# A hybrid decoder layer on one core: one tile of the input projection ahead of the first norm's spread

## The chip, the cores and the metric

The kernel runs on one core of one Trainium2 chip, as one program. The metric is the device time of one execution in microseconds (us). TensorE is called PE, VectorE DVE, ScalarE ACT, GpSimd POOL and SyncE SP.

## The reference, cut to what matters

One layer on 256 tokens of width 1024, in float32: a mixer whose three head groups read columns of one combined projection, then cross-attention to 256 memory tokens, then a gated feed-forward of width 2752 with a short convolution, and a last norm. The change touches the head and the tail of it:

```
def rmsnorm(x, g):
    xf = x.astype(jnp.float32)
    xf = xf * lax.rsqrt(jnp.mean(xf * xf, axis=-1, keepdims=True) + EPS)
    return xf.astype(x.dtype) * g
...
    proj = h @ w_in            # h = rmsnorm(x, norm_mix_g)
    (c_b, c_c, c_h, m_q, m_k, m_v, g_q, g_k, g_v, g_o, g_lr) = jnp.split(proj, points, axis=-1)
...
    return rmsnorm(x, final_norm_g)
```

## The kernel before, in words

Activations stand with features on the 128 partitions and the 256 tokens along the row. Each fp32 product is made from three: weights and activations are split into a high part (a cast to fp32r) and a low part (what is left), and PE adds high by high, high by low and low by high. ACT makes a weight's high part and DVE its low part (`emit_split`, lines 167 and 173; 162 and 163 where a piece is split in two halves).

All weights come as one stream of pieces in the order of `_stream_order`, loaded by `emit_load` on SP's queue into RAW = 6 raw buffers and split into PARTS = 4 pairs of buffers. The first eight pieces ("first", k) hold rows k of six column tiles of the input projection; PE works on all six at once, in the six PSUM tiles `first0` to `first5` (`fps`, line 295), while x arrives piece by piece. Pieces below HALVED = 3 are loaded, split and multiplied in two halves of 384 columns. The next pieces are single column tiles: ("in", MK+2P), here called in 1536 by its column, ("in", MQ+2P), in 1024, and then four "gla" pieces.

The norm's factor is not put into the operands; since it is one number per token, it is put into the results. It comes from a second load of x, token by token (`xtok`, 1 MB, line 237): ACT squares and sums it (line 345), `root_of` makes the root (lines 329, 330) and writes it on a diagonal (DVE, line 333), and `spread` (line 336) turns the diagonal with a matmul by ones into a row that every partition has, in the PSUM tile x_r, from which DVE copies it into `keep` (line 340). Only then can `scaled` (line 362) take a projection tile out of PSUM: `mk(0)` from first2, `mq(0)` from first3 and so on.

PSUM has eight banks here, in two tags, "ps" and "sd", of four each; `ps` (line 96) takes them by turns, and a new tile of a tag whose four banks are taken stands in the one that is released first. The warm-up tile, first0 to first5 and x_r take turns 1 to 8: warm, first1, first3 and first5 are "sd", first0, first2, first4 and x_r "ps". Then come in 1536 ("sd") and in 1024 ("ps").

A scheduler sets each engine's order from the program order and the dependencies, except where an instruction is pinned (`keep_in_program_order`, `manual_schedule`). Each engine and each DMA queue works in its order.

At the end, for each of two token tiles t, the last norm's factor r is put into the output row: DVE takes columns 512 to 1023 from PSUM (line 941), ACT columns 0 to 511 (line 944), each in two instructions of 256 columns, and SP and ACT each issue one store of 512 columns (line 946).

Of the kernel before, what the change touches and what calls it, by code (L numbers as in the profile page):

```python
# [14 lines left out]
AF = mybir.ActivationFunctionType  # L15
ALU = mybir.AluOpType
# [4 lines left out]
T = 256  # L21
D = 1024
KT = D // P
# [33 lines left out]

X_WITH = {1: (1, 2), 2: (2, 3), 3: (3, 4), 4: (4, 6), 6: (6, 8)}

HALVED = 3  # L60


def _stream_order():
# [14 lines left out]
def _width(key):  # L78
    return {"first": 768, "gla": 544}.get(key[0], 1024)
# [3 lines left out]
def trunk(ctx: ExitStack, tc: tile.TileContext, xT, x_rows, w_stream, params, gate, final, out):  # L83
    nc = tc.nc
    pe, act, dve, pool, sp = nc.tensor, nc.scalar, nc.vector, nc.gpsimd, nc.sync
# [10 lines left out]
    def ps(name):  # L96
        banks["turn"] += 1
        return pp.tile([P, 512], F32, tag=banks["tags"][banks["turn"] % len(banks["tags"])], name=name)

    def t1(name):  # L100
        return t1p.tile([P, T], F32, tag="t1", name=name)
# [18 lines left out]
    def emit_load():  # L120
        i = state["load"]
        state["load"] += 1
        key = order[i]
        t = rp.tile([P, SLOT], F32, tag="raw", name="w_" + "_".join(map(str, key)))
        if i == 0:

            act.dma_start(t[:, :384], w_stream[i, :, :384])
            load_x(0, 1)
            sp.dma_start(t[:, 384:768], w_stream[i, :, 384:768])
        else:  # L130
            if key[0] == "first" and key[1] in X_WITH:
                load_x(*X_WITH[key[1]])
            n = _width(key)
            step = n // 2 if i < HALVED else n
            for c in range(0, n, step):
                sp.dma_start(t[:, c:c + step], w_stream[i, :, c:c + step])
        raw[key] = t

    def emit_split(pin=False):
        i = state["split"]  # L140
        state["split"] += 1
        key = order[i]
        if key[0] == "mem":
            return
        n = _width(key)
        t = raw[key]
        if key in SPARE:
            tag = SPARE[key]
            if key[-1] == 0:
                spare[tag] = cp.tile([P, 4 * SLOT + 32], F32R, tag=tag, name="spare_" + tag)  # L150
            view = lambda c: spare[tag][:, ASIDE + c * SLOT:ASIDE + (c + 1) * SLOT]
            hi, lo = view(2 * key[-1]), view(2 * key[-1] + 1)
        elif key[0] == "dtail":
            hi = cp.tile([P, n], F32R, name="h_dtail")
            lo = lo_dtail
        else:
            at0 = 0 if key[0] in MOVING else ASIDE
            hi, lo = (hp.tile([P, SLOT + 32], F32R, tag=tag, name=tag[0] + "_" + "_".join(map(str, key)))[:, at0:at0 + n]
                      for tag in ("high", "low"))
        if i < HALVED:  # L160
            for c in (0, 384):
                act.copy(hi[:, c:c + 384], t[:, c:c + 384])  # L162
                dve.tensor_sub(lo[:, c:c + 384], t[:, c:c + 384], hi[:, c:c + 384])
            parts[key] = (hi, lo)
            return
        else:
            c = act.copy(hi, t[:, :n])  # L167
            if pin:
                tc.keep_in_program_order(c)
        if key[0] == "dtail":  # L170
            c = dve.tensor_sub(lo[:TAIL], t[:TAIL, :n], hi[:TAIL])
        else:
            c = dve.tensor_sub(lo, t[:, :n], hi)  # L173
        if pin:
            tc.keep_in_program_order(c)
        parts[key] = (hi, lo)

    def piece(*key):

        i = place[key]  # L180
        while state["load"] < min(len(order), i + RAW):
            emit_load()
        while state["split"] < min(len(order), i + 1 + AHEAD, state["until"]):
            emit_split()
        return raw[key] if key[0] == "mem" else parts[key]
# [31 lines left out]
    def feature_tile(dst, w, src, late=(), at=None, call=None):  # L217
        wb = blocks(w, P)
        ks = [k for k in range(KT) if k not in late]
        term = lambda k: ([a[:, k, :] for a in wb], [a[:, k, :] for a in src])  # L220
        todo = [(k, a, b) for g in (ks, late) for a, b in ((0, 0), (0, 1), (1, 0)) for k in g]
        for n, (k, a, b) in enumerate(todo):
            if n == at:
                call()
            s, m = term(k)
            pe.matmul(dst, s[a], m[b], start=(n == 0), stop=(n == len(todo) - 1))  # L226

    xt = cp.tile([P, PADDED + KT * T], F32, tag="res", bufs=2, name="x")
    x = xt[:, PADDED:].rearrange("p (k n) -> p k n", k=KT)
    emit_load()  # L230
    act.preload_act_table_set("natural_log_exp_and_others")
    for _ in range(KT - 1):
        emit_load()

    xtt = cp.tile([P, 4 * D], F32, tag="big", name="xtok")
# [9 lines left out]
    ones = cp.tile([P, P], F32, name="ones")  # L245
# [51 lines left out]
    with tc.manual_schedule(engines={mybir.EngineType.DVE}):  # L297
        for k in range(KT):
            state["until"] = place[("first", k)] + 1
            gained(xg, k, x[:, k, :], xt[:, k:k + 1], dve)  # L300
            w = piece("first", k)
            for some in ((range(3), range(3, 6)) if k < HALVED else (range(6),)):
                for a, b in ((0, 0), (0, 1), (1, 0)):
                    for i in some:
                        pe.matmul(fps[i][:, :T], w[a][:, i * P:(i + 1) * P], xg[b][:, k, :],  # L305
                                  start=(k == 0 and (a, b) == (0, 0)), stop=(k == KT - 1 and a == 1))
    state["until"] = place[("up", 0, 0)]

    def rstd_of(acc, name, features=True, tokens=False):


        m = ps(name + "_ms")
        got = []
        if features:
            pe.matmul(m[:, :T], ones, acc, start=True, stop=True)
            got.append((t1(name + "_r"), m[:, :T]))
        if tokens or not features:
            for j in range(2):
                pe.matmul(m[:, T + j:T + j + 1], acc[:, j * P:(j + 1) * P], ones[:, 0:1], start=True, stop=True)
            got.append((smp.tile([P, 2], F32, tag=name + "_rt", bufs=1, name=name + "_rt"), m[:, T:T + 2]))  # L320
        for r, q in got:
            act.activation(r, q, AF.Ln, bias=eps, scale=1.0)
            act.activation(r, r, AF.Exp, scale=-0.5)
        return [r for r, _ in got] if len(got) > 1 else got[0][0]

    def root_of(sums, name):

        rt = smp.tile([P, 2], F32, tag=name + "_rt", bufs=1, name=name + "_rt")
        act.activation(rt, sums, AF.Ln, bias=eps, scale=1.0 / D)
        act.activation(rt, rt, AF.Exp, scale=-0.5)  # L330
        diags = t1(name + "_diag")
        for j in range(2):
            dve.tensor_scalar(diags[:, j * P:(j + 1) * P], ident, rt[:, j:j + 1], float(D), op0=ALU.mult, op1=ALU.mult)
        return rt, diags

    def spread(r, diags, name):

        m = ps(name + "_r")
        pe.matmul(m[:, :T], ones, diags, start=True, stop=True)
        dve.tensor_copy(r, m[:, :T])  # L340

    xsum = small("x_sums")
# [3 lines left out]
    rt, diags = root_of(xsum, "x")  # L346
    keep = cp.tile([P, 2, T], F32, name="keep")
    rr, r = keep[:, 0, :], keep[:, 1, :]
    spread(r, diags, "x")


    for j in range(2):
# [15 lines left out]
    def dense(*key):  # L368
        q = ps("_".join(map(str, key)))
        feature_tile(q[:, :T], piece(*key), xg)  # L370
        return q[:, :T]
# [47 lines left out]
    def both(f, h):  # L419
        f(h)  # L420
        f(h + 1)

    both(bias_of, 0)
    q2 = dense("in", MK + 2 * P)
    gq, gk = t1("gq"), t1("gk")
    for i in range(2):
        scaled(mk(i), fps[2 + 2 * i][:, :T])
# [28 lines left out]
    for i in range(4):  # L456
        w = blocks(piece("gla", i), 272)
        for j in range(2):
            for a, b in ((0, 0), (1, 0), (0, 1)):
                for k in range(2):  # L460
                    pe.matmul(gps[j][:, :272], xg[a][:, 2 * i + k, j * P:(j + 1) * P], w[b][:, k, :],  # L461
                              start=(i == 0 and k == 0 and (a, b) == (0, 0)), stop=(i == 3 and k == 1 and b == 1))
# [135 lines left out]
    for n in (1, 2, 3):  # L598
        for c in range(2):
            ch = slice(64 * c, 64 * c + 64)  # L600
            pe.matmul(gos[c][:, 64 * n:64 * n + 64], st[ch, n, :], qd[ch, 64 * n:64 * n + 64],
                      start=False, stop=(n == 3), tile_position=(64 * c, 0))
# [157 lines left out]
    wps, acc = {}, {}  # L760
# [35 lines left out]
    gfin = cp.tile([P, D], F32, name="gfin")  # L796
# [58 lines left out]
    for j in range(NPAIR + 1):  # L855
        tail = j == NPAIR
        src = []
        for t in range(1 if tail else 2):
# [6 lines left out]
            elif t == 1:  # L865
# [3 lines left out]
                for k in range(KT):  # L869
                    for tt in range(2):  # L870
                        wb = blocks(piece("up", 0, tt), P)
                        for a, b in ((0, 0), (0, 1), (1, 0)):
                            pe.matmul(src[tt], wb[a][:, k, :], xg2[b][:, k, :], start=(k + a + b + tt == 0),
                                      stop=(k == KT - 1 and a == 1 and tt == 1))
# [4 lines left out]
                _, diags2 = root_of(tot2, "x2")  # L879
# [21 lines left out]
    fin = fint[:, :2 * D].rearrange("p (t n) -> p t n", t=2)  # L901
    half = fint[:, 2 * D:].rearrange("p (t n) -> p t n", t=2)
# [30 lines left out]
    for n, k, t in second:  # L933
        down(t, n, k)
        if k == NPAIR - 1:
            squares(t, 1)
            r = rs[:, t:t + 1]
            act.activation(r, sums[:, 2 * t + 1:2 * t + 2], AF.Ln, bias=bias[:, t:t + 1], scale=1.0 / D)
            act.activation(r, r, AF.Exp, scale=-0.5)
            for c in (512, 768):  # L940
                dve.scalar_tensor_tensor(fin[:, t, c:c + 256], acc[t, 1][:, c - 512:c - 256], r, gfin[:, c:c + 256],
                                         op0=ALU.mult, op1=ALU.mult)
            for c in (0, 256):
                act.activation(fin[:, t, c:c + 256], half[:, t, c:c + 256], AF.Copy, scale=r)
            for c, e in ((512, sp), (0, act)):
                e.dma_start(out[t * P:(t + 1) * P, c:c + 512], fin[:, t, c:c + 512])

# [99 lines left out]
```

## Time and profile before

| what | value |
|---|---|
| median of 3 runs | 330.21 us (330.07 to 331.2) |
| the profiled execution's own time | 330.21 us |
| its span, first to last instruction | 328.5 us |
| busy PE / DVE / ACT | 98% / 78% / 65% of the span |

The span is what the trace shows; the time has some 1.7 us around it. A row of the timeline gives the start, the time from there to the end of the last of its instructions, the engine and line, the operation, the tile written and the tiles read, and in brackets how long the engine sat idle before it and what ended that. A matmul's end is modelled, so PE's starts are what is read from it.

### The profile page before, as it was taken

The numbers are of one execution on the slowest core, as the hardware profiler recorded it, in microseconds if no ns is written. First come the engines' busy times: TensorE is split into PE (matmuls) and PEld (weight loads), VectorE is DVE, ScalarE is ACT, GpSimd is POOL, SyncE is SP. The second block draws the span as 40 slices with busy tenths as digits, with TensorE's granted clock in tenths as the row PEclk, the third lists the DMA queues.
The fourth block names the chain that finished last, engine by engine and source line by source line (L and its number), as shares of the span: only waits on it lengthen the run. The fifth ranks groups of instructions, "written<-read, shape, count | busy, mean of one in ns | idle before, by whom it ended". The sixth has DMA issues, their size and how long they took to land.

```text
span 328.5 us, 6408 instructions
## 1 busy us (share of the span) xinstructions
PE 320.3 (98%) x2462; PEld 296.2 (90%) x2462; DVE 257.2 (78%) x499; ACT 212.0 (65%) x393; POOL 2.7 (1%) x16
## 2 busy tenths in 40 slices
PE   8999999999999999999999999999999999999993
PEld 5999879898999998899999999999999988888882
DVE  7869879797998858588999999898989974444411
ACT  4675999566666756587886677666677653363323
POOL 3000000000000000000000000000000000000000
PEclk9999999999999999999999999999999999999999
DMA  7979953743378644207076866556558756552003
GB/s 218 401 302 323 325 188 89 247 177 131 130 234 274 198 130 129 66 0 257 0 224 229 272 228 203 194 192 195 193 192 246 210 182 200 192 191 66 0 0 128
DMA packets 18465, 60.38 MB, mean 184 GB/s; under 512 B 2034, under 2 KB 3459, under 8 KB 18435
## 3 DMA queue, kind: packets, MB, share of 16 engines
q1 hardware_dynamic: 18002, 59.26, 54.1%
q10 hardware_dynamic: 432, 0.72, 0.6%
q8 instruction: 19, 0.31, 0.4%
q14 instruction: 12, 0.09, 0.1%
HBM read 58.93 MB, written 1.05 MB: 183 GB/s over the span
## 4 chain that ended last, share of the span: by engine, by line
PE 85%; ACT 6%; DMA 4%; DVE 2%; issue 1%; SPq 0%; DVEq 0%; ACTq 0%
PE up L226 30%; PE dn L911 18%; PE in L226 10%; PE out L215 7%; PE v L477 3%; DMA xtok<-in_x_rows_dram 3%; PE gv L461 2%; PE xv L737 2%; PE wo L779 2%; PE xq L226 2%; PE xk L226 2%; ACT h_up L167 2%; DMA w_first<-in_w_stream_dram 1%; ACT hn L201 1%; PE et L404 1%; ACT x_sq L771 1%
## 5 line engine op out<-in xcount | busy, mean ns | idle before, releaser
L226 PE MATMUL up<-hn,h_up 128*128 128x256 f32 x576 | 71.2, 276 | 0.0
L226 PEld LDWEIGHTS up<-hn,h_up 128*128 128x128 f32 x576 | 68.0, 188 | 0.0
L167 ACT CAST h_up<-w_up 128x1024 fp32r<-128x1024 f32 x40 | 41.8, 1049 | 18.8 <-PE up L226 18.7
L911 PE MATMUL dn<-h_down,hid 128*128 128x512 f32 x168 | 52.8, 392 | 0.0
L173 DVE TENSOR_TENSOR l_up<-w_up,h_up 128x1024 fp32r<-128x1024 f32 x40 | 48.6, 1220 | 4.5 <-ACT h_up L167 3.6
L173 DVE TENSOR_TENSOR l_down<-w_down,h_down 128x1024 fp32r<-128x1024 f32 x21 | 25.7, 1225 | 25.2 <-ACT h_down L167 24.8
L167 ACT CAST h_down<-w_down 128x1024 fp32r<-128x1024 f32 x21 | 22.0, 1048 | 28.1 <-PE dn L911 25.2
L226 PE MATMUL up<-hn,l_up 128*128 128x256 f32 x288 | 38.6, 276 | 0.3 <-DVE l_up L173 0.3
L911 PEld LDWEIGHTS dn<-h_down,hid 128*128 128x128 f32 x168 | 31.6, 188 | 7.1
L226 PEld LDWEIGHTS up<-hn,l_up 128*128 128x128 f32 x288 | 35.4, 188 | 0.5 <-DVE l_up L173 0.5
L810 DVE SCALAR_TENSOR_TENSOR u<-up,par,u 128x255 f32<-128x255 f32 (+1 forms) x74 | 34.5, 476 | 0.5
L911 PE MATMUL dn<-l_down,hid 128*128 128x512 f32 x84 | 32.9, 392 | 0.0
L226 PE MATMUL in<-xg,h_in 128*128 128x256 f32 x192 | 25.0, 283 | 0.0
L226 PEld LDWEIGHTS in<-xg,h_in 128*128 128x128 f32 x192 | 23.0, 188 | 0.7 <-issue 0.5
L808 ACT ACTIVATE u<-up,par 128x256 f32<-128x256 f32 x37 | 20.5, 555 | 0.0
L911 PEld LDWEIGHTS dn<-l_down,hid 128*128 128x128 f32 x84 | 15.8, 188 | 3.5
L215 PE MATMUL out<-y,h_out 128*128 128x256 f32 x128 | 16.0, 277 | 0.0
L173 DVE TENSOR_TENSOR l_in<-w_in,h_in 128x1024 fp32r<-128x1024 f32 x12 | 14.6, 1220 | 1.7 <-ACT h_in L167 1.7
L215 PEld LDWEIGHTS out<-y,h_out 128*128 128x128 f32 x128 | 15.3, 188 | 0.0
L167 ACT CAST h_in<-w_in 128x1024 fp32r<-128x1024 f32 x12 | 12.4, 1044 | 3.9 <-issue 2.7
L305 PE MATMUL first<-xg,h_first 128*128 128x256 f32 x96 | 13.1, 280 | 0.8 <-ACT h_first L162 0.7
L305 PEld LDWEIGHTS first<-xg,h_first 128*128 128x128 f32 x96 | 11.8, 188 | 1.6 <-ACT h_first L162 1.3
(269 smaller groups left out, 543.6 us busy)
## 6 DMA issues: line engine op xcount, KB each, us to landing
w_up<-in_w_stream_dram SPq DMA_DIRECT2D x42, 512.0 KB, 3.4
w_down<-in_w_stream_dram SPq DMA_DIRECT2D x21, 512.0 KB, 3.3
w_in<-in_w_stream_dram SPq DMA_DIRECT2D x12, 512.0 KB, 4.7
w_out<-in_w_stream_dram SPq DMA_DIRECT2D x8, 512.0 KB, 3.4
w_mv<-in_w_stream_dram SPq DMA_DIRECT2D x4, 512.0 KB, 5.3
w_first<-in_w_stream_dram SPq DMA_DIRECT2D x5, 384.0 KB, 6.3
w_gla<-in_w_stream_dram SPq DMA_DIRECT2D x4, 272.0 KB, 6.7
xtok<-in_x_rows_dram SPq DMA_DIRECT2D x1, 1024.0 KB, 9.4
```

The lines of the kernel that those rows point to most:

```text
L167: c = act.copy(hi, t[:, :n])
L173: c = dve.tensor_sub(lo, t[:, :n], hi)
L215: pe.matmul(dst, s, m, start=(n == 0), stop=(n == len(todo) - 1))
L226: pe.matmul(dst, s[a], m[b], start=(n == 0), stop=(n == len(todo) - 1))
L305: pe.matmul(fps[i][:, :T], w[a][:, i * P:(i + 1) * P], xg[b][:, k, :], start=(k == 0 and (a, b) == (0, 0)), stop=(k == KT - 1 and a == 1))
L461: pe.matmul(gps[j][:, :272], xg[a][:, 2 * i + k, j * P:(j + 1) * P], w[b][:, k, :], start=(i == 0 and k == 0 and (a, b) == (0, 0)), stop=( ...
L477: pe.matmul(vps[j], xg[a][:, 2 * i + k, j * P:(j + 1) * P], w[b][:, k, :], start=(i == 0 and k == 0 and (a, b) == (0, 0)), stop=(i == 3 an ...
L737: pe.matmul(vps[j][:, :T], mg[a][:, 4 * i + k, j * P:(j + 1) * P], w[b][:, k, :], start=(i == 0 and k == 0 and (a, b) == (0, 0)), stop=(i ...
L779: pe.matmul(wps[o][:, :T], wb[a][:, 2 * (o % 4) + k, :], xo[b][:, k, :], start=(k == 0 and a + b == 0), stop=(k == 1 and a == 1))
L808: act.activation(v, src, AF.Identity, bias=fb(t), scale=fw(t, 2))
L810: dve.scalar_tensor_tensor(v[:, s:], src[:, :T - s], fw(t, 2 - s), v[:, s:], op0=ALU.mult, op1=ALU.add)
L911: pe.matmul(q, hid[i](k)[:, cols], w[j], start=False, stop=(k == NPAIR - 1 and i == 1), skip_group_check=True)
```

## The change

Four edits. The tile in 1536 is multiplied ahead of `spread`, whose matmul is now pinned to its place in the program; its weights are loaded ahead of `xtok` (nine loads are issued first, not eight) and split, pinned, ahead of the squares; HALVED is 4, so the fourth "first" piece is loaded, split and multiplied in halves; and the last results are written in one instruction of 512 columns on each engine.

```
-HALVED = 3
+HALVED = 4
...
-    for _ in range(KT - 1):
+    for _ in range(KT):
         emit_load()
...
     state["until"] = place[("up", 0, 0)]
+    emit_split(True)
...
-        pe.matmul(m[:, :T], ones, diags, start=True, stop=True)
+        tc.keep_in_program_order(pe.matmul(m[:, :T], ones, diags, start=True, stop=True))
...
-    spread(r, diags, "x")
...
     both(bias_of, 0)
     q2 = dense("in", MK + 2 * P)
+    spread(r, diags, "x")
...
-            for c in (512, 768):
-                dve.scalar_tensor_tensor(fin[:, t, c:c + 256], acc[t, 1][:, c - 512:c - 256], r, gfin[:, c:c + 256],
-                                         op0=ALU.mult, op1=ALU.mult)
-            for c in (0, 256):
-                act.activation(fin[:, t, c:c + 256], half[:, t, c:c + 256], AF.Copy, scale=r)
+            dve.scalar_tensor_tensor(fin[:, t, 512:], acc[t, 1], r, gfin[:, 512:], op0=ALU.mult, op1=ALU.mult)
+            act.activation(fin[:, t, :512], half[:, t, :], AF.Copy, scale=r)
```

On PE, from the last product of the first six tiles to the first scores, before (a name's number is its buffer; the tile behind the brackets' word is not told, only the engine whose semaphore is waited for):

```order
L305 MATMUL first5_165<-xg_159,l_first_7_355 128x256
L339 MATMUL x_r_387<-x_diag_383,ones_109 128x256 [waits DVE_49]
L226 MATMUL in_1536_398<-xg_159,h_in_1536_401 128x256 [waits Activation_49]
L226 MATMUL in_1536_398<-xg_159,h_in_1536_401 128x256 x15
L226 MATMUL in_1536_398<-xg_159,l_in_1536_402 128x256 [waits DVE_49]
L226 MATMUL in_1536_398<-xg_159,l_in_1536_402 128x256 x7
L226 MATMUL in_1024_447<-xg_159,h_in_1024_405 128x256 [waits DVE_49,Activation_49]
```

and now:

```order
L305 MATMUL first5_168<-xg_162,l_first_7_358 128x256
L226 MATMUL in_1536_402<-xg_162,h_in_1536_380 128x256 [waits Activation_49]
L226 MATMUL in_1536_402<-xg_162,h_in_1536_380 128x256 x15
L226 MATMUL in_1536_402<-xg_162,l_in_1536_381 128x256 [waits DVE_49]
L226 MATMUL in_1536_402<-xg_162,l_in_1536_381 128x256 x7
L340 MATMUL x_r_437<-x_diag_390,ones_112 128x256 [waits DVE_49,PE_49]
L226 MATMUL in_1024_450<-xg_162,h_in_1024_405 128x256 [waits DVE_49,Activation_49]
```

x_r's matmul has gone behind the 24 products of in 1536; in 1024 still waits for DVE, but its tile now has another predecessor in its bank. By the turns, in 1536 is now the fourth "ps" tile and x_r stands in the warm-up's "sd" bank, so in 1024 must take a "ps" bank from first0, first2, first4 or in 1536.

On DVE, from the last low part of the first pieces to the first scaled tiles, before:

```order
L173 TENSOR_TENSOR l_first_7_355<-w_first_7_101,h_first_7_354 128x768
L333 TENSOR_SCALAR x_diag_383<-ident_127,x_rt_380 128x128 x2
L173 TENSOR_TENSOR l_in_1536_402<-w_in_1536_248,h_in_1536_401 128x1024
L340 COPY keep_386<-x_r_387 128x256
L173 TENSOR_TENSOR l_in_1024_406<-w_in_1024_274,h_in_1024_405 128x1024
L173 TENSOR_TENSOR l_gla_0_410<-w_gla_0_300,h_gla_0_409 128x544
L364 TENSOR_TENSOR mix_392<-first2_162,keep_386 128x256
```

and now:

```order
L173 TENSOR_TENSOR l_first_7_358<-w_first_7_102,h_first_7_357 128x768
L173 TENSOR_TENSOR l_in_1536_381<-w_in_1536_104,h_in_1536_380 128x1024
L334 TENSOR_SCALAR x_diag_390<-ident_130,x_rt_387 128x128 x2
L173 TENSOR_TENSOR l_in_1024_406<-w_in_1024_277,h_in_1024_405 128x1024
L173 TENSOR_TENSOR l_gla_0_410<-w_gla_0_303,h_gla_0_409 128x544
L341 COPY keep_393<-x_r_437 128x256
L173 TENSOR_TENSOR l_gla_1_454<-w_gla_1_329,h_gla_1_453 128x544
L364 TENSOR_TENSOR mix_396<-first2_165,keep_393 128x256
```

The copy of x_r now stands behind the low parts of in 1024 and of the first gla piece, and the first scaled tile behind that of the second gla piece too.

On SP's queue, around the second load of x, before:

```order
L136 DMA w_first_7_101<-in_w_stream_dram 128x768
L237 DMA xtok_103<-in_x_rows_dram 128x2x1024
L239 DMA par_105<-in_params_dram 128x224
L241 DMA wg_107<-in_gate_dram 17x128
L136 DMA w_in_1536_248<-in_w_stream_dram 128x1024
```

and now:

```order
L136 DMA w_first_7_102<-in_w_stream_dram 128x768
L136 DMA w_in_1536_104<-in_w_stream_dram 128x1024
L237 DMA xtok_106<-in_x_rows_dram 128x2x1024
L239 DMA par_108<-in_params_dram 128x224
L241 DMA wg_110<-in_gate_dram 17x128
```

The 512 KB of in 1536 have gone ahead of xtok, the parameters and the gate's weights.

## Rows read from the trace of the kernel before

**Rows 1.** Page, part 1: busy time, share of the span, instructions.
```profile
PE 320.3 (98%) x2462; PEld 296.2 (90%) x2462; DVE 257.2 (78%) x499; ACT 212.0 (65%) x393; POOL 2.7 (1%) x16
```

**Rows 2.** PE's waits over the whole span: total us, times, longest.
```profile
PE warm L290 <- PEq L1035: 0.9, 1, 0.9
PE first L305 <- ACT h_first L162: 0.7, 1, 0.7
PE x_r L339 <- DVE x_diag L333: 0.4, 2, 0.2
PE up L226 <- DVE l_up L173: 0.3, 1, 0.3
```

**Rows 3.** Timeline of PE from 20.9 us.
```profile
21.11 0.84 PE L305 MATMUL first<-xg,l_first 128*128 128x256 f32 x6
22.15 0.70 PE L339 MATMUL x_r<-x_diag,ones 128*128 128x256 f32 x2 [0.19 <-DVE x_diag L333]
22.56 2.17 PE L226 MATMUL in<-xg,h_in 128*128 128x256 f32 x16
...
25.51 1.99 PE L226 MATMUL in<-xg,h_in 128*128 128x256 f32 x16
...
28.34 0.50 PE L385 MATMUL s<-mix 64*128 64x128 f32 x4
```

**Rows 4.** Timeline of ACT: x's second load has landed.
```profile
18.82 1.06 ACT L345 ACTIVATE xtok<-xtok 128x1024 f32<-128x1024 f32 x1 [2.21 <-DMA xtok<-in_x_rows_dram]
...
21.48 1.98 ACT L167 CAST h_in<-w_in 128x1024 fp32r<-128x1024 f32 x2
```

**Rows 5.** Timeline of DVE from 22.5 us.
```profile
22.54 1.22 DVE L173 TENSOR_TENSOR l_in<-w_in,h_in 128x1024 fp32r<-128x1024 f32 x1 [0.45 <-ACT h_in L167]
23.68 0.42 DVE L340 COPY keep<-x_r 128x256 f32<-128x256 f32 x1
24.02 1.22 DVE L173 TENSOR_TENSOR l_in<-w_in,h_in 128x1024 fp32r<-128x1024 f32 x1
25.15 0.72 DVE L173 TENSOR_TENSOR l_gla<-w_gla,h_gla 128x544 fp32r<-128x544 f32 x1
25.79 0.42 DVE L364 TENSOR_TENSOR mix<-first,keep 128x256 f32<-128x256 f32 x1
26.12 0.41 DVE L366 SCALAR_TENSOR_TENSOR mix<-first,keep 128x256 f32<-128x256 f32 x1
```

**Rows 6.** Stretches: length, PE, PEld, DVE, ACT, POOL busy; PEclk, DMA share, GB/s.
```profile
4.00:8.80 4.80, 4.08 (x34) 3.95 (x34) 4.51 (x12) 2.89 (x6) 0.00 (x0) 1.00 0.97 294
...
14.00:18.80 4.80, 4.80 (x45) 4.80 (x44) 4.70 (x10) 1.71 (x3) 0.00 (x0) 1.00 1.04 416
```

**Rows 7.** Timeline of ACT and of PE around the fourth piece.
```profile
10.58 0.83 ACT L167 CAST h_first<-w_first 128x768 fp32r<-128x768 f32 x1 [1.64 <-DMA w_first<-in_w_stream_dram]
...
10.89 0.50 PE L305 MATMUL first<-xg,l_first 128*128 128x256 f32 x3
11.47 1.65 PE L305 MATMUL first<-xg,h_first 128*128 128x256 f32 x12
```

**Rows 8.** The tail's timeline, and three groups of instructions (busy us, mean ns).
```profile
324.04 0.91 ACT L944 ACTIVATE fin<-fin,x_r 128x256 f32<-128x256 f32 x2
324.04 0.88 DVE L941 SCALAR_TENSOR_TENSOR fin<-dn,x_r,gfin 128x256 f32<-128x256 f32 x2 [3.25 <-ACT x_r L939]
...
L932 DVE TENSOR_TENSOR fin<-dn,gfin 128x512 f32<-128x512 f32 x2 | 1.4, 681 | 0.0
L503 ACT ACTIVATE mix<-v,x_rt 128x512 f32<-128x512 f32 x2 | 1.2, 669 | 0.0
L465 ACT ACTIVATE gv<-gv,x_rt 128x256 f32<-128x256 f32 x2 | 0.9, 461 | 0.0
```

**Rows 9.** Timeline of PE, the warm-up.
```profile
0.85 3.22 PE L290 MATMUL warm<-const-bfloat16-1.0 128*128 128x512 bf16 x8 [0.85 <-PEq L1035]
```

## The prediction

> **What bounds the kernel now.** I read the share of busy time first: PE is busy for 98% of the span, DVE for 78%, ACT for 65% [rows 1]. Then PE's own waits [rows 2]: apart from the start there are two, 0.4 us for the norm's diagonal (two records, 0.2 the longest) and 0.3 us once for a low part. So PE bounds nearly everything, a microsecond that PE loses near the head has nothing behind it that would give it back, and the change can win at most the small gap in front of x_r and something in the tail. That gap is read from starts [rows 3]: the last six products of the first tiles start at 21.11, and at 24 products in 2.83 us (25.51 to 28.34), 0.118 each, PE could go on at 21.82; x_r starts at 22.15. The gap is 0.33 us. What x_r waits for begins with xtok: ACT's squares start when it lands, at 18.82 [rows 4].
>
> A change of 0.5%, 1.65 us, is about what a measurement of this kernel can tell from none.
>
> **The fourth piece by halves.** PE runs out of the third piece's products at 10.89 + 3 × 0.118 = 11.24 and starts the fourth at 11.47, when ACT's cast of 0.83 us from 10.58 is done [rows 7]: 0.23 us that halves could save, since half a cast is enough to begin. One more issue on SP, one more cast and one more subtraction are the price; SP's later loads are each issued one place later, behind full DMA engines (share 0.97 and 1.04) [rows 6], so that issue is covered as long as these are full. The load's rows are half as long. The stretch in which halves and short rows of x are loaded moves 294 GB/s, the one with whole pieces 416 [rows 6]: for 393 KB that is 1.34 against 0.94 us, so the halving delays all that follows by 0 to 0.4 us; most of the first stretch's shortfall may be x's shorter rows, so I take 0.15. The Trainium skill (DMA: Bandwidth & Descriptors, "Why small descriptors are slow (HBM only)") states a fixed cost of about 3 cycles beside one cycle for each 32 bytes; by that my estimate of the delay would be 0.03 us, 102 cycles for 99, and the time 0.1 us less. No row here separates the two.
>
> **The projection tile ahead of the spread.** PE then goes on at about 21.6 with in 1536 (the 0.23 us of the fourth piece taken off 21.82), needs 2.83 us, and x_r's matmul (0.41 us, 22.15 to 22.56) follows, to about 24.8. Its weights are there: the last first piece is cast at about 15.7, 512 KB more at 416 GB/s land some 1.3 us behind it, at about 17.2; ACT idles for 2.21 us before 18.82 [rows 4] and takes the cast, DVE the low part at the end of its first pieces. So this step does what it says, and the gap of 0.33 us is closed. If nothing else happened, PE would be ahead.
>
> **What the load's new place costs.** xtok goes behind 524,288 bytes in SP's queue. The engines are full there [rows 6], so it lands 524,288 / 416 GB/s = 1.26 us later, plus 0.15 from the halves: 18.80 + 1.41 = 20.21. Bounds: no delay at all if the engines took transfers side by side, and 1.26 + 0.4 = 1.66 us. I take the sum, since a full set of engines leaves no room. The parameters and the gate's weights move with xtok, and no wait on PE stands for them [rows 2]; the loads behind, in 1024's first, have the same bytes ahead of them as before.
>
> **The wait that takes the gap's place.** in 1024 is the next tile on PE. Before, it stood in x_r's bank, free when DVE had copied x_r (23.68 + 0.42 = 24.10 [rows 5]), long before PE came to it at 25.51, so PE did not stop [rows 3]. Now x_r stands in the warm-up's bank, and in 1024 needs a bank of the other four: first0, first2, first4 and in 1536, none of which can be read before r is in `keep`. The first to be read is first2, by the first scaled tile. So in 1024 can't start before DVE has copied x_r *and* scaled first2, and both now stand behind low parts of weights that are not yet needed. Worked out from xtok's landing, by starts of rows: to the first low part after the root 22.54 − 18.82 = 3.72 [rows 4, 5] (the cast of in 1024 now comes where that of in 1536 was); the low part of in 1024 takes 1.13 (24.02 to 25.15), of a gla piece 0.64 (25.15 to 25.79), the copy 0.34 (23.68 to 24.02), the second gla piece 0.64, the scaled tile 0.42 and its signal 0.06 (as from the cast's end, 10.58 + 0.83, to PE's 11.47 [rows 7]): 3.23 us. in 1024 starts at 20.23 + 3.72 + 3.23 = 27.18, where before it started at 25.51. **PE is 1.67 us later there**, and idle for about 2.4 us from 24.8. Both gains further up (0.23 and 0.33 us) go into that idle time and are worth nothing. Even with xtok on time the wait would end at 25.77.
>
> Behind it nothing more is late: the scores of the first heads need mq(0), 0.33 us after first2 [rows 5], and in 1024's own 2.83 us cover that; DVE's remaining scalings run beside it; the low parts of the later gla pieces were made after the scores' first pass and now partly ahead of it; ACT's casts and the softmax move with PE. As PE waits hardly anywhere after this [rows 2], the 1.67 us reach the end.
>
> **The tail.** ACT's two instructions take 0.91 us and DVE's two 0.88 [rows 8]. One of 512 columns takes ACT 0.67 where it scales so elsewhere (461 ns for 256 columns), and DVE 0.68 [rows 8]: 0.24 and 0.20 less. Each store starts that much earlier; the later of the two counts, and it shares the transfer engines with the other. I take 0.15, between nothing and 0.2. The first token tile's results lie beside PE's last products.
>
> **Sum.** The profiled execution took 330.21 us, which is the median of the runs too. 330.21 + 1.67 − 0.15 = **331.7 us**. With the bounds for the halves (0 and 0.4) and 0.2 either way for DVE's chain, this case spans 331.4 to 332.2.
>
> **Rivals.**
> 1. *The clock falls.* PE has not been idle for over 0.9 us in this trace [rows 2], and the granted clock reads 1.00 in every stretch [rows 6]; after 2.4 us of nothing it might not. The warm-up's eight products of 512 columns took 3.22 us, 0.40 each [rows 9], which is near the lower of the two levels, 1.2 of 2.4 GHz. If a stretch as long as the warm-up ran at half rate, 1.6 us are lost: 333.3. It decides if the granted clock falls in the stretch from 27 us. The Trainium skill (TensorE: Matmul & The Clock Gate, "HAM oscillation — how this bites in real kernels") describes just this: waits between bursts take the clock back and the next burst starts slow. Against it stands that one idle stretch in a busy kernel is all there is. No run here shows such a fall.
> 2. *xtok is not delayed*: the wait then ends at 25.77, 0.26 us later than before, less the tail: 330.3. Against it, the full engines.
> 3. *The bank is no wait*, because another tile's bank is used. Then in 1024 starts at 24.8 and ends at 27.6; the scores need mq(0), which DVE has at 27.18 + 0.33, so they start at 27.6, 0.7 us earlier than the 28.34 of before: 330.21 − 0.7 − 0.15 = 329.3. This is the one on the other side, faster though by less than 0.5%. For it speaks only that the turns are counted, not traced; against it, that PE still waits for DVE ahead of in 1024 in the new order.
> That in 1536 is split too late for its place would not matter to the time: the wait ends by DVE's chain from xtok.
>
> **How the numbers follow.** Forecast 0.76, rival 1 0.12, rivals 2 and 3 0.06 each. The forecast's middle lies 1.5 us over before, just under 1.65; I put 0.34 of its 0.76 above that line. Slower: 0.34 + 0.12 = 0.46. Same: 0.42 + 0.06 + 0.06 = 0.54, of which I give 0.02 to faster for a third rival larger than worked out: 0.52 and 0.02. The range takes in rival 2 at its low end and rival 1 at its high end with a little over: 330.3 to 333.4; rival 3 and longer falls of the clock are left out.
>
> **What would show it.** xtok's squares start near 20.2, x_r's matmul near 24.4, in 1024 near 27.2 with PE idle before it for over 2 us, released by DVE's scaling of first2; the fourth piece starts at 11.24; each final instruction is one of 0.7 us. I am wrong if PE goes straight from x_r to in 1024, if the squares still start near 18.8, or if PE catches up later.

## The result, and the profile after

The kernel with the change takes 333.78 us (median of 4 runs, 333.14 to 334.68), the kernel before on the same chip 330.14 (4 runs, 329.41 to 331.2): a ratio of 1.0105 with a 95% interval of 1.0081 to 1.013. It is slower by 3.6 us, and the time lies 0.4 us above the range. The profiled execution took 333.71 us, its span is 332.0.

PE's waits, of the kernel after (total us, times, longest), against [rows 2]:

```profile
PE in L226 <- DVE mix L364: 2.6, 1, 2.6
PE warm L290 <- PEq L1034: 0.8, 1, 0.8
PE first L305 <- ACT h_first L162: 0.6, 1, 0.6
...
```

One new wait has come, of 2.6 us, in front of a tile of the projection, and DVE's scaling ends it; the other two were there before. PE's timeline after, against [rows 3]:

```profile
20.69 0.84 PE L305 MATMUL first<-xg,l_first 128*128 128x256 f32 x6
21.37 1.98 PE L226 MATMUL in<-xg,h_in 128*128 128x256 f32 x16
...
24.10 0.59 PE L340 MATMUL x_r<-x_diag,ones 128*128 128x256 f32 x2
27.30 3.54 PE L226 MATMUL in<-xg,h_in 128*128 128x256 f32 x16 [2.61 <-DVE mix L364]
30.64 1.25 PE L226 MATMUL in<-xg,l_in 128*128 128x256 f32 x8
31.82 0.50 PE L385 MATMUL s<-mix 64*128 64x128 f32 x4
```

Two things have happened to in 1024. It starts at 27.30, where it was 25.51: 1.79 us later. And its 24 products take 31.82 − 27.30 = 4.52 us, where they took 2.83: 1.69 us more. Together the first scores are 3.48 us late. The stretches of one microsecond from 24 (columns as in [rows 6]) tell why the products are slow:

```profile
24.00:25.00 1.00, 0.69 (x5) 0.29 (x3) 1.00 (x1) 1.00 (x3) 0.00 (x0) 1.00 0.08 33
25.00:26.00 1.00, 0.00 (x0) 0.00 (x0) 1.00 (x3) 0.60 (x2) 0.00 (x0) 1.00 0.04 16
26.00:27.00 1.00, 0.00 (x0) 0.00 (x0) 1.00 (x3) 0.00 (x0) 0.00 (x0) 1.00 0.64 156
27.00:28.00 1.00, 0.70 (x4) 0.73 (x5) 1.00 (x4) 0.00 (x0) 0.00 (x0) 0.78 0.96 315
28.00:29.00 1.00, 1.00 (x7) 1.00 (x6) 1.00 (x4) 0.00 (x0) 0.00 (x0) 0.50 1.02 414
...
30.00:31.00 1.00, 1.00 (x6) 1.00 (x6) 0.11 (x1) 0.12 (x1) 0.00 (x0) 0.52 0.85 340
31.00:32.00 1.00, 1.00 (x10) 0.87 (x10) 0.07 (x1) 0.53 (x1) 0.00 (x0) 1.00 0.52 143
```

Follow the column with PEclk, the one after the five engines. It reads 1.00 while PE stands idle, falls when PE has gone on, is 0.50 (1.2 of 2.4 GHz) to nearly 31, and 1.00 again from 31. In a stretch at 0.50 PE does 6 or 7 products, at 1.00 ten, the first scores among them. So in this run the price of the idle stretch is paid after it.

Where the wait comes from stands in ACT's and DVE's rows, against [rows 4, 5]:

```profile
20.27 1.06 ACT L346 ACTIVATE xtok<-xtok 128x1024 f32<-128x1024 f32 x1 [2.52 <-DMA xtok<-in_x_rows_dram]
```

```profile
24.00 1.23 DVE L173 TENSOR_TENSOR l_in<-w_in,h_in 128x1024 fp32r<-128x1024 f32 x1 [0.45 <-ACT h_in L167]
25.14 0.72 DVE L173 TENSOR_TENSOR l_gla<-w_gla,h_gla 128x544 fp32r<-128x544 f32 x1
25.77 0.42 DVE L341 COPY keep<-x_r 128x256 f32<-128x256 f32 x1
26.11 0.72 DVE L173 TENSOR_TENSOR l_gla<-w_gla,h_gla 128x544 fp32r<-128x544 f32 x1
26.74 0.42 DVE L364 TENSOR_TENSOR mix<-first,keep 128x256 f32<-128x256 f32 x1
```

xtok comes 1.45 us later than before. x_r is done at about 24.7, but DVE copies it at 25.77, behind the low parts of in 1024 and of a gla piece, and frees a bank for in 1024 at 26.74 + 0.42, behind another one.

The tail, against [rows 8]; first PE's last matmul and the last store's issue before, then the rows now:

```profile
322.33 0.39 PE L911 MATMUL dn<-h_down,hid 128*128 128x512 f32 x1
...
324.98 0.36 ACTq L946 DMA_DIRECT2D out_dram<-fin  x1
```

```profile
325.80 0.39 PE L913 MATMUL dn<-h_down,hid 128*128 128x512 f32 x1
...
327.51 0.72 ACT L943 ACTIVATE fin<-fin,x_r 128x512 f32<-128x512 f32 x1
327.51 0.75 DVE L942 SCALAR_TENSOR_TENSOR fin<-dn,x_r,gfin 128x512 f32<-128x512 f32 x1 [3.38 <-ACT x_r L941]
328.26 0.36 ACTq L945 DMA_DIRECT2D out_dram<-fin  x1
```

The last results take 0.75 us where they took 0.91, so the later of the two is done 0.16 us sooner, about as forecast. From PE's last matmul (322.33 before, 325.80 after) the store by ACT's queue is issued after 2.65 us before and 2.46 after. But from that same matmul to the execution's own time there are 7.88 us before and 7.91 after: the 0.19 us are gone by the end.

### The profile page after: what moved, and what is told of

It is laid out like the page before. It is cut to its first block, busy times and chain, and to the rows that moved or that the text cites. A ratio compares the mean times of both kernels' runs of the same rounds, so it can differ in the third digit from the quotient of the medians.

```text
span 332.0 us, 6408 instructions
## 1 busy us (share of the span) xinstructions
PE 321.5 (97%) x2462; PEld 297.5 (90%) x2462; DVE 257.1 (77%) x498; ACT 212.1 (64%) x392; POOL 2.7 (1%) x16
## 3 DMA queue, kind: packets, MB, share of 16 engines
HBM read 58.93 MB, written 1.05 MB: 181 GB/s over the span
## 4 chain that ended last, share of the span: by engine, by line
PE 84%; ACT 6%; DMA 5%; DVE 3%; issue 1%; SPq 0%; DVEq 0%; ACTq 0%
PE up L226 30%; PE dn L913 17%; PE in L226 10%; PE out L215 7%; PE v L479 3%; DMA xtok<-in_x_rows_dram 3%; DMA w_first<-in_w_stream_dram 2%; PE gv L463 2%; PE xv L739 2%; PE wo L781 2%; PE xq L226 2%; PE xk L226 2%; ACT h_up L167 2%; ACT hn L201 1%; PE et L404 1%
## 5 line engine op out<-in xcount | busy, mean ns | idle before, releaser
L226 PE MATMUL in<-xg,h_in 128*128 128x256 f32 x192 | 26.4, 293 | 2.6 <-DVE mix L364 2.6
L226 PEld LDWEIGHTS in<-xg,h_in 128*128 128x128 f32 x192 | 24.3, 198 | 3.6 <-issue 3.5
L226 PE MATMUL in<-xg,l_in 128*128 128x256 f32 x96 | 13.2, 280 | 0.0
```

## Experiments

The theory is the one of the prediction with rival 1 in it: the load's new place and DVE's order make the wait, the idle time brings the clock down, and both reach the end. Rival theories were that the halves cost something, that the delayed load is itself the price, and that the products from 27.30 are slow for another reason than the clock (DMA is at work beside them).

**1. Halves and 512-column results alone** (the kernel before with the two small edits).

```
-HALVED = 3
+HALVED = 4
...
+            dve.scalar_tensor_tensor(fin[:, t, 512:], acc[t, 1], r, gfin[:, 512:], op0=ALU.mult, op1=ALU.mult)
+            act.activation(fin[:, t, :512], half[:, t, :], AF.Copy, scale=r)
```

> Only the fourth piece by halves and the results in 512s. Theory (a wait for a PSUM bank in front of the tile in 1024, and TensorE's clock falling in that wait, make the loss): neither is here, x_r starts within 0.2 us of before's 22.15, in 1024 within 0.2 us of 25.51, the granted clock reads 1.00 everywhere, time 330.0 to 330.4. Rival (the halved loads or the longer last instructions cost a part of the loss): 331 or more.

Measured: 329.96 us against 330.29, ratio 0.9987 [0.9978, 0.9996]. The order of work is that of before, and in the profiled execution all of it comes 0.47 us earlier (x_r at 21.68 where it was 22.15, scores at 27.85 where they were 28.34), which is more than the 0.2 us that I allowed. So these edits do no harm alone.

```profile
20.97 0.84 PE L305 MATMUL first<-xg,l_first 128*128 128x256 f32 x6
21.68 0.70 PE L339 MATMUL x_r<-x_diag,ones 128*128 128x256 f32 x2
```

Six products from 20.97 last until 21.68, and x_r starts there: the gap in front of x_r, which the reorder was to close, is already gone in this profile. xtok's squares start at 18.35 in it, 0.47 us earlier than before too; whether the halves did that or the one execution, these profiles can't tell.

**2. The reorder alone** (the kernel before with the load, the tile and the pinned spread moved), run twice.

```
-    for _ in range(KT - 1):
+    for _ in range(KT):
...
+    emit_split(True)
...
-        pe.matmul(m[:, :T], ones, diags, start=True, stop=True)
+        tc.keep_in_program_order(pe.matmul(m[:, :T], ones, diags, start=True, stop=True))
...
-    spread(r, diags, "x")
...
     q2 = dense("in", MK + 2 * P)
+    spread(r, diags, "x")
```

> Only the tile in 1536 and its load ahead, HALVED and the last results as before. Theory: all of the loss is here; PE is idle for some 2.3 us before in 1024, which starts at 27.1 to 27.3, the granted clock falls to half for over 3 us there, time 333.3 to 333.9. Rival (the halves or the tail cost): 332.5 or less.

> The reorder without the halves and without the 512-column results, once more, because its first profile had a late transfer for the second piece. Theory (without the halves TensorE comes later to a wait whose end x's second load fixes, so that the idle stretch is shorter): idle stretch of 1.6 to 2.2 us ahead of in 1024, clock 1.00 in most runs, 331.8 to 332.3, that is 1.5 us under the change. Rival (the two runs differed by the chip or by that late transfer alone): clock falls, 333.5 to 334.

Measured: first 332.22 us, ratio 1.0058 [1.0042, 1.0075], then 333.60, ratio 1.0088 [1.0064, 1.0112]. PE's timeline and a later stretch of the first profile, then of the second:

```profile
27.85 2.08 PE L226 MATMUL in<-xg,h_in 128*128 128x256 f32 x16 [1.74 <-DVE mix L364]
29.77 1.07 PE L226 MATMUL in<-xg,l_in 128*128 128x256 f32 x8
```

```profile
29.00:30.00 1.00, 1.00 (x12) 1.00 (x11) 1.00 (x5) 0.03 (x1) 0.00 (x0) 1.00 0.88 320
```

```profile
27.15 2.71 PE L226 MATMUL in<-xg,h_in 128*128 128x256 f32 x16 [1.96 <-DVE mix L364]
29.66 1.91 PE L226 MATMUL in<-xg,l_in 128*128 128x256 f32 x8
```

```profile
29.00:30.00 1.00, 1.00 (x7) 1.00 (x6) 0.96 (x2) 0.10 (x1) 0.00 (x0) 0.50 0.88 299
```

In the first, a late transfer for the second piece of weights had held PE up before (1.6 us of waits on its casts), so PE reached the wait later, idled for 1.74 us, and the clock held. In the second it idled for 1.96 us, and the granted clock was 0.68 in 28:29 and 0.50 from 29 to 31. After the first run it looked as if the halves, harmless alone, made the difference, because with them PE comes earlier to a wait whose end xtok fixes. The second run takes that away: without the halves the clock falls too. They bring PE earlier to the wait, but they don't decide. By its times the same kernel seems to have done both: 331.92 to 332.60 us four times on the first chip, 332.29 once and 333.47 to 334.71 three times on the second. The rival that I named, that the two chips differ, is not ruled out by this pair; the one short time on the second chip speaks against the chip alone.

**3. The bank alone.** The change, but x_r's tile is taken from PSUM ahead of in 1536, so that in 1024 has x_r's bank and waits for the copy only, not for the first scaled tile.

```
+    m_x = ps("x_r")
     q2 = dense("in", MK + 2 * P)
-    spread(r, diags, "x")
+    spread(r, diags, "x", m_x)
```

> The changed kernel, but x_r's PSUM tile is taken ahead of in 1536's, so that in 1024 again follows x_r in its bank and waits for DVE's copy alone. DVE's order is that of the changed kernel, where the copy ends at 26.19: in 1024 starts at 26.2 instead of 27.30, PE idle for 1.7 instead of 2.6 us. Theory with a clock that holds through the shorter idle time: 0.7 us over before, 330.9. Theory with a clock that falls all the same: 332.4. Rival (in 1024's products are slow for another reason than the clock, such as transfers beside them): granted clock 1.00 and the products still at twice their spacing, 332.4.

Measured: 331.14 us, ratio 1.0031 [1.0019, 1.0043].

```profile
24.05 0.59 PE L340 MATMUL x_r<-x_diag,ones 128*128 128x256 f32 x2
26.25 2.12 PE L226 MATMUL in<-xg,h_in 128*128 128x256 f32 x16 [1.60 <-DVE keep L341]
28.20 1.10 PE L226 MATMUL in<-xg,l_in 128*128 128x256 f32 x8
29.24 0.50 PE L385 MATMUL s<-mix 64*128 64x128 f32 x4
```

in 1024 starts 1.05 us earlier than in the change, and its 24 products take 2.99 us. The bank is worth 1.05 us of wait by itself and, since the clock holds after 1.60 us, 2.6 us in all by the medians, which come from different runs and perhaps different chips.

**4. Useless work in the idle time.** The change with 22 products of constants behind the spread.

```
+    for _ in range(FILL):
+        tc.keep_in_program_order(pe.matmul(q2t[:, T:], heat[:, :P], heat[:, :T], start=True, stop=True))
```

> The changed kernel with 22 products of constant ones, 256 columns each, in the unused half of in 1536's bank, between x_r and in 1024: PE works through its wait, which is as long as it was (in 1024 at 27.3). Theory: the granted clock stays at 1.00, in 1024's 24 products take 2.8 us, not 4.5, and the time is that of the wait alone, 331.9 to 332.2. Rival (the products are slow for another reason): 333.6 to 333.9, as the changed kernel. 22 more products are computed and not used.

Measured: 332.28 us, ratio 1.0068 [1.0052, 1.0083].

```profile
24.78 2.63 PE L434 MATMUL in<-const-bfloat16-1.0 128*128 128x256 bf16 x22
27.65 2.07 PE L228 MATMUL in<-xg,h_in 128*128 128x256 f32 x16 [0.24 <-DVE mix L366]
29.55 1.07 PE L228 MATMUL in<-xg,l_in 128*128 128x256 f32 x8
30.55 0.50 PE L389 MATMUL s<-mix 64*128 64x128 f32 x4
```

```profile
28.00:29.00 1.00, 1.00 (x12) 1.00 (x11) 1.00 (x4) 0.00 (x0) 0.00 (x0) 1.00 0.94 361
```

in 1024 starts even later than in the change (27.65), and yet the scores start 1.27 us earlier, because the products take 2.90 us at a clock of 1.00, beside the same scalings on DVE and the same transfers (361 GB/s here, 414 in the change). This rules out contention: the slow products were the clock, and what differs is that PE had been idle. A kernel that does 2.6 us of useless work is 1.5 us faster by the medians than one that waits. One rival is left by this experiment alone: experiments 1 to 4 (the first run of 2) ran on one chip, no profile from it shows a fall, and no run of the change is on record as made on it, so the chip may have held the clock. Two other chips answer that. On the one of experiments 5, 7 and 8 the clock was 0.50 behind 2.50 us of idle time and 1.00 behind 0.61 us and behind none; on the one of experiments 6, 9 and 10 it was 0.50 behind 2.70 us and 1.00 behind none. With the products of experiment 4, the idle time is what is left as the cause.

**5. A little useless work** (the kernel of experiment 4 with 4 such products).

```
-FILL = 22
+FILL = 4
```

> The change with 4 added products of constants (bf16, 256 columns, into the unused half of tile in 1536's bank; nothing reads them) behind the spread, about 0.47 us of TensorE's time, so that the idle stretch ahead of in 1024 is about 2.1 us instead of 2.6. Theory (the length of the idle stretch in one piece decides, between the 1.74 us after which the clock held and the 2.61 after which it fell): the clock holds, in 1024 near 27.3 takes 2.8 us, time near 332.1. Rival (what decides is the light load of the whole stretch from 24 on): granted clock 0.50 again, in 1024 takes 4.5 us with its second half, time near 333.7.

Measured: 334.05 us in the median, but the five runs are 331.48, 331.82, 334.05, 334.68 and 335.42, ratio 1.0101 [1.0065, 1.0137]. In the profiled one xtok landed late (its squares start at 21.99), PE idled for 2.50 us before in 1024, and the clock was 0.50 from 31 to 33. Theory and rival each gave one time (332.1 and 333.7), and times on either side appear. At about this idle time the same kernel seems to hold its clock in one run and not in the next, probably because xtok's landing moves; only the slowest of the five has a profile, so this is not shown.

**6. Cutting the idle time in two.** 4 products that read the low part of the first gla piece were to stand in the middle of the wait.

```
+        w = piece(*key)
+        if fill is not None:
+            for _ in range(FILL):
+                tc.keep_in_program_order(pe.matmul(fill[:, T:], xg[0][:, 0, :P], parts[("gla", 0)][1][:, :T],
+                                                   start=True, stop=True))
...
```

The edit also pins the products of in 1024, of the scores and of the gla pieces to the program's order.

> The change with 4 added products (fp32r, 256 columns, into the unused half of tile in 1536's bank; nothing reads them) that read the difference l_gla which VectorE writes in the middle of TensorE's idle stretch, so that this stretch is cut into two of about 1.1 and 1.0 us, where the 4 products right behind the spread left one of 2.1 to 2.5. Theory (the length of one piece decides): clock 1.00 in all runs, in 1024 takes 2.8 us, time near 332.1. Rival (the idle time in all decides): the clock falls in about as many runs as with the 4 products behind the spread (3 of 5), median near 333.5.

Measured: 337.30 us, ratio 1.0197 [1.0178, 1.0216]. The experiment failed as such: the added products wrote into the bank of in 1536, and so waited for DVE to read that tile first:

```profile
30.18 1.22 PE L377 MATMUL in<-l_gla,xg 128*128 128x256 f32 x4 [4.84 <-DVE mix L368]
```

```profile
29.00:30.00 1.00, 0.00 (x0) 0.00 (x0) 1.00 (x4) 0.00 (x0) 0.00 (x0) 0.50 0.93 344
```

It gives one more length instead: with 4.84 us of idle time the clock was 0.50 from 29 to 35, twice as long as in the change. Here it fell while PE still stood idle (0.50 in 29:30, PE going on at 30.18), so a fall does not need PE to go on first. Whether the longest piece or the sum of idle time counts stays open.

**7. The load alone** (the kernel before, nine loads ahead of xtok instead of eight).

```
-    for _ in range(KT - 1):
+    for _ in range(KT):
```

> The kernel before with the ninth load ahead of x's second load, and nothing else of the change. Theory (the load alone is free, because tile in 1536 has its weights earlier and fills the time for which x's second load is late): x's second load seen by ScalarE near 20.1, the spread near 23.4, in 1024 near 25.4, clock 1.00, time 330.0 to 330.4. Rival (the delayed second load is itself the price, 1.3 us of it at in 1024): in 1024 near 26.8, time 331.4; with the clock falling as well 333.

Measured: 330.43 us, ratio 1.0006 [0.9996, 1.0016].

```profile
20.27 1.06 ACT L345 ACTIVATE xtok<-xtok 128x1024 f32<-128x1024 f32 x1 [2.37 <-DMA xtok<-in_x_rows_dram]
```

```profile
21.89 1.41 PE L226 MATMUL in<-xg,h_in 128*128 128x256 f32 x11
23.60 0.70 PE L339 MATMUL x_r<-x_diag,ones 128*128 128x256 f32 x2 [0.30 <-DVE x_diag L333]
23.95 0.94 PE L226 MATMUL in<-xg,h_in 128*128 128x256 f32 x5
24.72 1.10 PE L226 MATMUL in<-xg,l_in 128*128 128x256 f32 x8
25.70 2.06 PE L226 MATMUL in<-xg,h_in 128*128 128x256 f32 x16
```

xtok is as late as in the change, and it costs nothing that can be measured: with the spread not pinned, the scheduler puts x_r into the middle of in 1536, whose other 13 products cover the copy, and in 1024 keeps x_r's bank by the turns. The delayed load is not the price.

**8. The change without the wait.** Two versions: bank first, copy pinned early, the next low part pinned behind it; in the second the spread also stands behind 18 of in 1536's 24 products.

```
+    m_x = ps("x_r")
+    state["until"] = place[("in", MK + 2 * P)] + 1
...
+    feature_tile(q2[:, :T], piece("in", MK + 2 * P), xg, (), 18, lambda: spread(r, diags, "x", m_x))
```

> The change with three things undone of what it brought to the engines: the spread's PSUM tile x_r is taken before tile in 1536's, so that in 1024 waits only for the copy of the spread; that copy is pinned; and the split of the next load's cast (the VectorE subtraction that stood ahead of the copy) is pinned behind it. Theory (the load alone costs nothing where the tile covers it; the 2.6 us wait came from the bank and from the order of VectorE's work, and the slow clock from that wait): spread near 24.1, copy done near 25.2, in 1024 near 25.3 (before 25.51), less than 1.3 us of idle time ahead of it, granted clock 1.00 from 20 to 35, time 329.9 to 330.3. Rival (the load moved ahead costs by itself, wherever the spread goes): in 1024 not before 26, time 330.9 or more.

> The change with the spread's product put inside tile in 1536, behind 18 of its 24 products, its PSUM tile taken first, its copy pinned and the next split pinned behind the copy. Theory (the path is second load, root, spread, copy, in 1024; nothing of tile in 1536 needs to stand ahead of the spread but what covers the late load): spread near 23.5, copy done near 24.6, in 1024 near 24.8 or, if the split of its weights is the later, near 25.2, clock 1.00, time 329.2 to 329.7, which is faster than the kernel before and than the halves and 512-column results alone (329.96). Rival (the copy is behind other VectorE work and gives nothing back): in 1024 near 25.4, time 330.0 to 330.3.

Measured: 330.57 us, ratio 1.0013 [1.0003, 1.0023], and 329.96 us, ratio 0.9992 [0.9982, 1.0002]. In the profile of the first, in 1024 starts 3.93 us after in 1536 (22.48 to 26.41): 24 products (2.83), x_r (0.41), and 0.69 us for the way from x_r over DVE's copy to PE, which nothing covers. in 1024 is 1.1 us later than theory said, as in 1536 is against the change, in an execution that took 331.23 us; the median lies between theory's time and the rival's. In the second:

```profile
22.15 1.98 PE L226 MATMUL in<-xg,h_in 128*128 128x256 f32 x16
23.96 0.39 PE L226 MATMUL in<-xg,l_in 128*128 128x256 f32 x2
24.19 0.59 PE L342 MATMUL x_r<-x_diag,ones 128*128 128x256 f32 x2
24.43 1.05 PE L226 MATMUL in<-xg,l_in 128*128 128x256 f32 x6
25.39 2.12 PE L226 MATMUL in<-xg,h_in 128*128 128x256 f32 x16
```

From 22.15 to 25.39 it is 3.24 us, just the products and x_r: PE waits for nothing. It still misses the 329.2 to 329.7 that I expected, since in 1536 started at 22.15, not at the 21.37 of the change: in this run, which took 330.30 us, PE's earlier pieces came later. What the reorder could win is the 0.33 us gap, and no more, and experiment 1's profile had no such gap left. At 329.96 this version and that of experiment 1 take the same time; that of experiment 1 is the simpler, and its 0.13% is clear of no change by its interval, though under the 0.5% from which the prediction counted a change.

**9. The 512-column results alone** (the kernel before with this edit).

```
-            for c in (512, 768):
-                dve.scalar_tensor_tensor(fin[:, t, c:c + 256], acc[t, 1][:, c - 512:c - 256], r, gfin[:, c:c + 256],
-                                         op0=ALU.mult, op1=ALU.mult)
...
+            dve.scalar_tensor_tensor(fin[:, t, 512:], acc[t, 1], r, gfin[:, 512:], op0=ALU.mult, op1=ALU.mult)
```

> The kernel before with the results in 512s, alone. Theory (the two stores of the last tile issue 0.15 us earlier by the engines' rows, but their landing at the end moved by nothing in the change's profile, so the 0.4 us that halves and 512s gave together came from the halves): time equal to the kernel before within 0.1 us, ratio 0.9997 to 1.0003. Rival (the forecast's term: 0.15 us less): 330.1, ratio 0.9995.

Measured: 330.72 us against 330.45, ratio 1.0002 [0.999, 1.0014]; the rival's 0.9995 lies inside the interval, so the times don't decide. The profiles do, by the time from PE's last matmul to the execution's end: 7.88, 7.85, 7.85 and 7.85 us with two instructions each (before, experiment 7 and both of 2), and 7.79 to 7.94 in the profiles with one. The term is nothing that can be seen. By subtraction what is left of experiment 1 is the halves'; no run has them alone.

**10. The change once more**, without an edit.

> The change itself once more, beside the next three. Theory (x's second load lands at 20 to 22 by the run, the idle stretch ahead of in 1024 is 2.3 to 3 us, and after that the clock falls): 333.1 to 334.7 in nearly all runs, granted clock near 0.5 within 28 to 31. If the fall is a matter of chance at this length, single runs of 331.5 to 332 appear.

Measured: 333.94 us (333.14 to 334.19), ratio 1.0096 [1.0078, 1.0113]. In its profile PE idled for 2.70 us, the clock was 0.50 from 29 to 32, and in 1024 took 4.15 us.

Put side by side, each from one profiled execution:

| kernel | idle before in 1024, us | lowest clock | in 1024's 24 products, us | scores start | own time less that start |
|---|---|---|---|---|---|
| before | none | 1.00 | 2.83 | 28.34 | 301.87 |
| halves, 512s (1) | none | 1.00 | 2.81 | 27.85 | 301.71 |
| spread in the middle (8) | none | 1.00 | 3.00 | 28.39 | 301.91 |
| load alone (7) | none | 1.00 | 2.90 | 28.60 | 301.84 |
| 512s alone (9) | none | 1.00 | 2.83 | 28.57 | 301.78 |
| 22 useless products (4) | 0.24 | 1.00 | 2.90 | 30.55 | 301.89 |
| bank and copy put right (8, first) | 0.61 | 1.00 | 2.91 | 29.32 | 301.91 |
| bank alone (3) | 1.60 | 1.00 | 2.99 | 29.24 | 301.92 |
| reorder alone, first (2) | 1.74 | 1.00 | 2.92 | 30.77 | 301.83 |
| reorder alone, second (2) | 1.96 | 0.50 | 4.35 | 31.50 | 301.97 |
| 4 useless products (5) | 2.50 | 0.50 | 4.40 | 33.43 | 301.99 |
| the change | 2.61 | 0.50 | 4.52 | 31.82 | 301.89 |
| the change again (10) | 2.70 | 0.50 | 4.15 | 31.67 | 302.22 |

The last column is the point of the table. From the first scores on, every one of these kernels takes 301.7 to 302.2 us. What was lost before the scores is not given back behind them, and next to nothing is lost there; in the last row the clock was still 0.81 in 32:33, behind the scores' start, which is its 0.3 us.

## Why the prediction was wrong

Point by point, forecast and profile after:

- *Fourth piece by halves*: forecast to start at 11.24; it starts at 11.17 without a wait. Right. The delay that I put on it, 0.15 us from between 0 and 0.4, does not show: xtok's squares start at 20.27 with the load and the halves, and at 20.27 with the load alone (experiment 7), and the halves without the load have them at 18.35, not behind the 18.82 of [rows 4]. The estimate of 0.03 us from the Trainium skill (DMA: Bandwidth & Descriptors, "Why small descriptors are slow (HBM only)") lies nearer to that, but the squares move by more than 0.15 us from one profile to the next, so no run here separates the two.
- *xtok's landing*: forecast 1.41 us later, measured 1.45. Right in size, and in these profiles the load ahead makes all of it, where I had 1.26 from the load and 0.15 from the halves. It is also looser than one row shows: over the profiles with the load ahead the squares start between 20.11 and 21.99.
- *PE goes straight on with in 1536*: forecast about 21.6, measured 21.37. Right.
- *The wait*: forecast 27.18, released by DVE's scaling of first2; measured 27.30, released by it. Right, and experiment 3 shows the bank's part, 1.05 us.
- *The tail*: forecast 0.15 us less, measured nothing. The engines' part came about as forecast, and by the end it was gone; why, no run tells.
- *Behind it nothing more is late*: right for DVE, ACT and the loads, as the table's last column shows, and wrong for PE itself.

**The step that failed** is the sum's silent term that in 1024 takes 2.83 us wherever it stands: that the granted clock holds. I had it as rival 1, with the right mechanism, the right trigger (the stretch from 27 us) and a price of 1.6 us that is near the 1.69 measured, and gave it a chance of 0.12. The sum with the measured terms is 330.21 + 1.79 + 1.69 + 0.03 (tail) = 333.72, and the profiled execution took 333.71. Rival 1's own time, 333.3, was 0.4 short of that: 0.12 by the wait, 0.09 by the slow products and 0.18 by the tail, which had been taken off and did not come. That its price was so near is in part luck: it took the warm-up's length for that of the slow stretch, for which no row spoke; over the warm-up itself the trace's granted clock reads 1.00, so that it ran slow is read from its 0.40 us alone; and in experiment 6 the slow stretch was twice as long as in the change. The reason that I put against it, that one idle stretch in a busy kernel is all there is, was no reason from a row: the trace of before has no idle time of this length on PE, so it could not say that the clock would hold through one. The section that I named of the Trainium skill (TensorE: Matmul & The Clock Gate, "HAM oscillation — how this bites in real kernels") describes the rival's mechanism, and the trace agrees with it: 0.50 behind the idle time. The waits in that section's example are longer than this one, though, so it did not describe just this case, as I wrote. With a bound that no row supports from either side, the two cases should have had near equal chances, and the range should have reached past 333.4.

## What to carry to other kernels

When a change adds an idle stretch of two microseconds or more to a TensorE that is otherwise hardly idle, count the wait and then, as a term of its own, slow products behind it: here 1.79 and 1.69 us. Before moving a tile, follow what its new neighbours wait for: here a pool that hands out PSUM banks by turns gave the next tile a bank that is free only when the copy and a scaling are done, where the old one was free after the copy, and a copy of 0.4 us stood behind weight splits that nobody needed yet. A transfer that comes 1.45 us later was free as long as products stood on both sides of its consumer; with the consumer behind the whole tile 0.69 us stood open even with bank and copy put right (experiment 8), and 2.61 us with neither.

## What the runs showed of the hardware

- After one idle stretch of PE of 1.96 to 2.70 us the granted clock fell to 0.50 in each of the four profiles that have one, and in all four it fell only after PE had resumed, so that the idle time itself reads 1.00; with 4.84 us of idle time it fell within it. After 1.60 and 1.74 us it held, both on one chip; the kernel of the 1.74 us is the one that fell after 1.96 us on another. There is no clean border: with 4 useless products the runs of one kernel fall into 331.5 to 331.8 and 334.1 to 335.4. I take the second group for runs in which the clock fell; only one of them has a profile.
- With the last two stores issued 0.12 and 0.19 us earlier the execution ended no earlier, counted from PE's last matmul, in ten profiles against four. In the two profiles of before and after, the store on SP's queue lands 2.3 us after its issue before and 2.7 us after, the one on ACT's 2.6 us in both. Why, no run here tells.
